# Seven products of a Strassen-like block product: matmuls alternate between two weight matrices and the halves of one PSUM bank

## The chip, the cores and the metric

The kernel runs on one core of a Trainium2 chip. The metric is the device time of one execution in microseconds (us). Two executions of the kernel before are shown: 1855.19 and 1855.77 us, median 1855.48 us. TensorE (PE) multiplies, ScalarE (ACT), VectorE (DVE) and GpSimd (POOL) do the elementwise work, and SyncE (SP) issues nearly all loads.

## The reference

A two-layer decoder trunk for 512 positions of width 1024 in float32. Each layer is a half-weighted SwiGLU block, a mixer (attention of three kinds), and another half-weighted SwiGLU block:

```
h = h + 0.5 * swiglu(rmsnorm(h, g[0]), w1, w3, w2)     # (silu(x @ w1) * (x @ w3)) @ w2
h = h + mixer(rmsnorm(h, g[1]))
h = h + 0.5 * swiglu(rmsnorm(h, g[2]), w1, w3, w2)
```

So there are four SwiGLU blocks. Their hidden width is 2816, which is 22 tiles of 128. The change lies in the products `x @ w1` and `x @ w3` of 18 of these 22 tiles.

## The kernel before

**Numbers.** Every float32 operand is split into a high part and a low part (fp32r), and each product is three matmuls: low weight by high input, high weight by low input, high weight by high input.

**Tiling of a SwiGLU block** (`ffn`, L628). The 22 hidden tiles come in three parts of 8, 8 and 6. After each part, eight second-layer units (`w2`) are multiplied (L366 to L368). The first four tiles of the first part go through `gate` (L439), with plain 512-column matmuls. The others are taken two at a time by `gates` (L562): a pair of tiles needs a two by two block product, which is done with seven smaller products in place of eight. So a block has 2 + 4 + 3 = 9 pairs, and the kernel has 36.

**One pair.** `sevens` (L519) loads four raw tiles, `one` and `two` for w1 and for w3 (L541, L542, both through L328), and makes the weights of the seven products from them. For w1 and then for w3: a11 with a12 (one 1024-wide split), a22 (a 512-wide split), then, after four additions at L533, s2 with s4, and s3 with s1 (1024-wide each). A split is a cast on ACT (L336) and a subtraction on DVE (L315), so a pair makes eight of each, in the order just told. The raw tiles and the split weights share 20 buffers, and a load on SP waits until its buffer is free.

**The seven products** (`product`, L571). In the order a11, a12, s2, s1, s3, s4, a22 each multiplies the weights of w1 into columns 0 to 255 of a PSUM bank and the weights of w3 into columns 256 to 511. Each half is one operation of the planner: 12 matmuls of 256 columns (four steps k of three). The bank is read (L594, L597) when both halves are done. `normed` (L458) makes the inputs of the products once for each block.

**What sets the order.** `Plan.emit` (L172) is a list scheduler that runs when the program is built. Each operation has an engine, a cost in ns, the tiles that it reads and writes, and a due value `v`; of the operations that could start soonest on an engine, the one with the smallest `v` goes next. An operation is offered only when all that it reads has been planned. The result is one fixed order for each engine; at run time every instruction waits for its own operands, and an engine runs its list strictly in order.

Of the kernel before, what the change touches and what calls it, by code (L numbers as in the profile page):

```python
# [103 lines left out]
def vec_ns(n):  # L104
    return n / 0.96 + 155


def sca_ns(n, extra=0):
    return n / 1.2 + 190 + 93 * extra
# [158 lines left out]
class Trunk:  # L268
# [293 lines left out]
    def gates(self, l, n, f, sx):  # L562


        nc, t = self.nc, self.t
        ws = self.sevens([(t[m][l, n, f], t[m][l, n, f + 1]) for m in ("w1", "w3")])
        pa, pb, pc = self.bank("sa"), self.bank("sb"), self.bank("sk")
        q1, q2 = Buf("d4", "cq2", (128, 1024)), Buf("d4", "cq2", (128, 1024))
        first, second = slice(0, 256), slice(256, 512)

        def product(ps, left, right, start):  # L571
            for m in range(2):
                w, c0 = ws[m][left]

                def g(m=m, w=w, c0=c0):
                    o = ps.t[:, m * 256:m * 256 + 256]
                    for k in range(4):
                        h, l, c, _ = sx[right][k]
                        at = slice(c0 + k * 128, c0 + k * 128 + 128)
                        wh, wl, xh, xl = w.at(0, at), w.at(1, at), h.t[:, c], l.t[:, c]  # L580
                        nc.tensor.matmul(o, wl, xh, start=start and m == 0 and k == 0, stop=False, skip_group_check=True)  # L581
                        nc.tensor.matmul(o, wh, xl, start=False, stop=False, skip_group_check=True)  # L582
                        nc.tensor.matmul(o, wh, xh, start=False, stop=k == 3, skip_group_check=True)  # L583
                keys = [key for x in sx[right] for key in x[3]]
                self.pe(12 * 117.5, g, self.parts(w) + keys, [ps])

        def view(q, c):
            return q.t.rearrange("p (m s) -> p m s", m=2)[:, :, c]

        def bank(ps):  # L590
            return ps.t.rearrange("p (m s) -> p m s", m=2)

        def copy(q, c, ps, key):
            self.act(sca_ns(S) - 40, lambda: nc.scalar.copy(view(q, c), bank(ps)), [ps], [(q, key)])  # L594

        def add(q, c, ps, key):
            self.dve(vec_ns(S), lambda: nc.vector.tensor_add(view(q, c), bank(ps), view(q, c)), [ps, (q, key)], [(q, key)])  # L597
        product(pa, "a11", "b11", True)
        copy(q1, first, pa, 0)
        product(pb, "a12", "b21", True)  # L600
        add(q1, first, pb, 0)
        product(pa, "s2", "t2", False)
        copy(q1, second, pa, 1)
        product(pc, "s1", "t1", True)
        copy(q2, second, pc, 1)
        product(pa, "s3", "t3", False)
        add(q2, second, pa, 1)
        product(pc, "s4", "b22", False)
        add(q1, second, pc, 1)
        product(pa, "a22", "t4", False)  # L610
        copy(q2, first, pa, 0)
        out = []
        for q, sign in ((q1, 1.0), (q2, -1.0)):
            g = self.s2("fa")
            gh, gl = self.s2("gt", F32R), self.s2("gt", F32R)
            self.act(sca_ns(S), lambda q=q, g=g, sign=sign: nc.scalar.activation(
                g.t, q.t[:, :512], AF.Silu, scale=sign), [(q, 0), (q, 1)], [g])
            if sign > 0:
                self.dve(vec_ns(S), lambda q=q, g=g: nc.vector.tensor_mul(g.t, g.t, q.t[:, 512:]), [g, (q, 0), (q, 1)], [g])
            else:  # L620
                self.dve(vec_ns(S), lambda q=q, g=g: nc.vector.scalar_tensor_tensor(
                    g.t, q.t[:, 512:], -1.0, g.t, op0=OP.mult, op1=OP.mult), [g, (q, 0), (q, 1)], [g])
            self.act(sca_ns(S), lambda g=g, gh=gh: nc.scalar.copy(gh.t, g.t), [g], [gh])
            self.sub(lambda gl=gl: gl.t, lambda g=g: g.t, lambda gh=gh: gh.t, [g, gh], [gl], S, ns=vec_ns)
            out.append((gh, gl))
        return out
# [695 lines left out]
```

## Time and profile before

| what | value |
|---|---|
| median of the two executions | 1855.48 us |
| the profiled execution, its own time | 1856.36 us |
| its span, first to last instruction | 1854.6 us |
| PE busy / DVE busy / ACT busy / POOL busy | 98% / 75% / 50% / 13% |
| mean granted TensorE clock | 0.99 of 2.4 GHz |
| matmuls at L581, L582, L583 | 2016 each, 128x256, 6048 in all |
| HBM traffic | 102 GB/s over the span |

A matmul's listed duration (about 283 ns) overlaps with the next ones; the distance between two starts is what one costs in a full stream. "Idle before" and "releaser" tell how long an engine stood still before an instruction and which event ended that. The profiled execution's own time is 1.8 us above its span and 0.9 us above the median.

### The profile page before, as it was taken

What the parts mean: (1) busy time and instruction counts of PE and PEld (TensorE: products, weight loads), DVE (VectorE), ACT (ScalarE), POOL (GpSimd) and SP (SyncE); (2) the same over time, 40 slices, a digit from 0 to 9 for tenths busy, and PEclk for the clock granted to TensorE, in tenths of its full rate; (3) what the DMA queues carried; (4) which work ended last, traced back from release to release, by engine and by line L of the source; (5) the groups of instructions that cost most, each with busy time, mean ns of one, the idle gap of its engine ahead of it and who ended that gap; (6) DMA issues with size and microseconds to landing.
All of it is one profiled execution on the core that took longest, in us unless ns stands there. A gap on an engine that the chain in (4) does not pass through costs nothing.

```text
span 1854.6 us, 28373 instructions
## 1 busy us (share of the span) xinstructions
PE 1811.5 (98%) x11174; PEld 1619.7 (87%) x11178; DVE 1398.2 (75%) x2222; ACT 936.2 (50%) x1558; POOL 245.1 (13%) x240
## 2 busy tenths in 40 slices
PE   8899999989999999999999999999999999999997
PEld 6789989867877789899998989989888889899896
DVE  7965866759998898487588965857789898567483
ACT  6443533636757746254264543525569655345153
POOL 1500001024622120010001000001023120010010
PEclk9899999999999999999999999999999999999999
DMA  6463233432222323234334223323412223243131
GB/s 210 121 207 101 84 101 106 126 103 77 87 59 78 93 71 121 62 108 132 91 103 125 69 91 103 125 70 103 137 60 69 86 80 95 78 124 126 60 112 46
DMA packets 65431, 185.45 MB, mean 100 GB/s; under 512 B 11985, under 2 KB 14769, under 8 KB 65297
## 3 DMA queue, kind: packets, MB, share of 16 engines
q1 hardware_dynamic: 58176, 176.88, 30.9%
q0 software_dynamic: 6688, 6.66, 1.3%
q8 instruction: 87, 1.43, 0.3%
q14 instruction: 48, 0.39, 0.1%
q10 hardware_dynamic: 432, 0.10, 0.0%
HBM read 179.81 MB, written 8.47 MB: 102 GB/s over the span
## 4 chain that ended last, share of the span: by engine, by line
PE 81%; DVE 12%; issue 2%; ACT 2%; DMA 2%; POOL 1%; SPq 1%; DVEq 0%; POOLq 0%; ACTq 0%
PE ps L581 12%; PE ps L582 12%; PE ps L583 12%; PE ps L366 11%; PE ps L367 11%; PE ps L368 11%; DVE d L315 3%; DVE s L315 2%; PE ps L837 1%; DMA d<-in_w 1%; PE ps L839 1%; PE ps L838 1%; PE ps L797 1%; DVE s L755 1%; DVE s L471 1%
## 5 line engine op out<-in xcount | busy, mean ns | idle before, releaser
L336 ACT CAST d<-d 128x1024 fp32r<-128x1024 f32 (+4 forms) x492 | 448.6, 927 | 405.0 <-DMA d<-in_w 223.3
L315 DVE TENSOR_TENSOR d<-d,d 128x1024 fp32r<-128x1024 f32 (+3 forms) x475 | 507.1, 1084 | 176.1 <-ACT d L336 155.0
L581 PE MATMUL ps<-s,d 128*128 128x256 f32 x2016 | 572.2, 284 | 10.9 <-DVE d L315 7.9
L582 PE MATMUL ps<-s,d 128*128 128x256 f32 x2016 | 571.5, 283 | 0.0
L583 PE MATMUL ps<-s,d 128*128 128x256 f32 x2016 | 571.4, 283 | 0.0
L366 PE MATMUL ps<-s,d 128*128 128x512 f32 x1188 | 471.8, 397 | 3.6 <-DVE d L315 3.6
L367 PE MATMUL ps<-s,d 128*128 128x512 f32 x1188 | 465.1, 392 | 0.2
L368 PE MATMUL ps<-s,d 128*128 128x512 f32 x1188 | 464.7, 391 | 0.0
L581 PEld LDWEIGHTS ps<-s,d 128*128 128x128 f32 x2016 | 388.0, 192 | 12.5 <-DVE d L315 8.2
L582 PEld LDWEIGHTS ps<-s,d 128*128 128x128 f32 x2016 | 388.0, 192 | 0.5
L583 PEld LDWEIGHTS ps<-s,d 128*128 128x128 f32 x2016 | 387.9, 192 | 0.0
L366 PEld LDWEIGHTS ps<-s,d 128*128 128x128 f32 x1188 | 224.4, 189 | 47.9 <-DVE d L315 3.8
L368 PEld LDWEIGHTS ps<-s,d 128*128 128x128 f32 x1188 | 224.0, 189 | 47.8
L367 PEld LDWEIGHTS ps<-s,d 128*128 128x128 f32 x1188 | 224.5, 189 | 42.9 <-DVE s L315 0.5
L594 ACT COPY d<-ps 128x512 f32<-128x512 f32 x144 | 84.4, 586 | 217.6 <-PE ps L583 217.5
L653 DVE SCALAR_TENSOR_TENSOR s<-ps,s 128x512 f32<-128x512 f32 x88 | 60.7, 690 | 137.0 <-PE ps L368 136.8
L315 DVE TENSOR_TENSOR s<-s,s 128x512 fp32r<-128x512 f32 (+2 forms) x188 | 148.7, 803 | 7.3 <-ACT s L372 2.1
L533 POOL TENSOR_TENSOR d<-d 128x512 f32<-128x512 f32 x18 | 23.6, 1313 | 937.1 <-DVE d L533 807.1
L597 DVE TENSOR_TENSOR d<-ps,d 128x512 f32<-128x512 f32 x108 | 73.5, 686 | 32.7 <-PE ps L583 32.1
L533 DVE TENSOR_TENSOR d<-d,d 128x512 f32<-128x512 f32 x133 | 87.5, 686 | 1.7
L533 DVE TENSOR_TENSOR d<-d 128x512 f32<-128x512 f32 x126 | 85.6, 695 | 2.2
L764 ACT ACTIVATE s<-s,stat 128x256 f32<-128x256 f32 (+3 forms) x128 | 65.9, 516 | 24.6 <-DVE stat L755 23.9
(147 smaller groups left out, 1872.0 us busy)
## 6 DMA issues: line engine op xcount, KB each, us to landing
d<-in_w SPq DMA_DIRECT2D x234, 512.0 KB, 3.7
d<-in_w SPq DMA_DIRECT2D x32, 384.0 KB, 3.2
d<-in_hyb_in SPq DMA_DIRECT2D x22, 512.0 KB, 3.9
d<-in_swa_in SPq DMA_DIRECT2D x10, 512.0 KB, 3.6
tab<-rv POOLq DMA_DIRECT2D x4, 1024.0 KB, 16.7
s<-tab SPq DMA_DIRECT2D x16, 256.0 KB, 4.0
d<-in_hyb_out SPq DMA_DIRECT2D x16, 256.0 KB, 2.9
d<-in_swa_out SPq DMA_DIRECT2D x16, 256.0 KB, 2.7
```

The source lines that it names most:

```text
L315: return lambda: eng.tensor_sub(out(), a(), b().bitcast(F32))
L336: alts = [("act", ns[0](n), lambda: nc.scalar.copy(hl.at(0, o), raw.t[:, c]))]
L366: nc.tensor.matmul(o, wl, xh.t, start=i == 0, stop=False)
L367: nc.tensor.matmul(o, wh, xl.t, start=False, stop=False)
L368: nc.tensor.matmul(o, wh, xh.t, start=False, stop=i == n - 1)
L533: return lambda: eng.tensor_add(o.t[:, oc], a.t[:, ac], o.t[:, oc])
L581: nc.tensor.matmul(o, wl, xh, start=start and m == 0 and k == 0, stop=False, skip_group_check=True)
L582: nc.tensor.matmul(o, wh, xl, start=False, stop=False, skip_group_check=True)
L583: nc.tensor.matmul(o, wh, xh, start=False, stop=k == 3, skip_group_check=True)
L594: self.act(sca_ns(S) - 40, lambda: nc.scalar.copy(view(q, c), bank(ps)), [ps], [(q, key)])
L597: self.dve(vec_ns(S), lambda: nc.vector.tensor_add(view(q, c), bank(ps), view(q, c)), [ps, (q, key)], [(q, key)])
L764: nc.scalar.activation(x, x, AF.Exp, bias=st.t[:, qb:qb + 1], scale=-1.0, accum_out=st.t[:, 4 + qb:5 + qb])
```

## The change

The two operations of a product become one of 24 matmuls. Within each step k, and for each of the three kinds, a matmul with w1 into the first half of the bank is followed by one with w3 into the second half. The number of matmuls, their shapes and operands stay. Each half still gets its 12 matmuls in the same order, and the flag that starts a bank stands on the first matmul alone, as before. The operation's cost is the sum of the two, and it reads the split weights of w1 and of w3.

```diff
         def product(ps, left, right, start):
-            for m in range(2):
-                w, c0 = ws[m][left]
-
-                def g(m=m, w=w, c0=c0):
-                    o = ps.t[:, m * 256:m * 256 + 256]
-                    for k in range(4):
-                        h, l, c, _ = sx[right][k]
-                        at = slice(c0 + k * 128, c0 + k * 128 + 128)
-                        wh, wl, xh, xl = w.at(0, at), w.at(1, at), h.t[:, c], l.t[:, c]
-                        nc.tensor.matmul(o, wl, xh, start=start and m == 0 and k == 0, stop=False, skip_group_check=True)
-                        nc.tensor.matmul(o, wh, xl, start=False, stop=False, skip_group_check=True)
-                        nc.tensor.matmul(o, wh, xh, start=False, stop=k == 3, skip_group_check=True)
-                keys = [key for x in sx[right] for key in x[3]]
-                self.pe(12 * 117.5, g, self.parts(w) + keys, [ps])
+            both = [ws[m][left] for m in range(2)]
+
+            def g():
+                for k in range(4):
+                    h, l, c, _ = sx[right][k]
+                    xh, xl = h.t[:, c], l.t[:, c]
+                    for a, x in ((1, xh), (0, xl), (0, xh)):
+                        for m, (w, c0) in enumerate(both):
+                            nc.tensor.matmul(ps.t[:, m * 256:m * 256 + 256], w.at(a, slice(c0 + k * 128, c0 + k * 128 + 128)), x,
+                                             start=start and m == 0 and k == 0 and a == 1, stop=k == 3 and a == 0 and x is xh,
+                                             skip_group_check=True)
+            keys = [key for x in sx[right] for key in x[3]]
+            self.pe(24 * 117.5, g, [key for w, _ in both for key in self.parts(w)] + keys, [ps])
```

## Rows read from the trace of the kernel before

**Rows 1.** Page, part 1: engine, busy us, share of the span, instructions.
```profile
PE 1811.5 (98%) x11174; PEld 1619.7 (87%) x11178; DVE 1398.2 (75%) x2222; ACT 936.2 (50%) x1558; POOL 245.1 (13%) x240
```

**Rows 2.** Page, part 4: the chain that ended last, share of span by engine.
```profile
PE 81%; DVE 12%; issue 2%; ACT 2%; DMA 2%; POOL 1%; SPq 1%; DVEq 0%; POOLq 0%; ACTq 0%
```

**Rows 3.** Page, part 5: line, operation, count, busy us, mean ns, idle before, releaser.
```profile
L581 PE MATMUL ps<-s,d 128*128 128x256 f32 x2016 | 572.2, 284 | 10.9 <-DVE d L315 7.9
...
L583 PE MATMUL ps<-s,d 128*128 128x256 f32 x2016 | 571.4, 283 | 0.0
```

**Rows 4.** Waits: who waited for whom, us in total, times, longest.
```profile
PE ps L581 <- DVE d L315: 7.9, 1, 7.9
```

**Rows 5.** Stretches: length, busy us (count) of PE, PEld, DVE, ACT, POOL, clock, DMA.
```profile
777.80:797.96 20.16, 20.16 (x170) 20.15 (x168) 8.62 (x13) 5.42 (x8) 1.30 (x1) 1.00 0.47 148
...
59.70:63.80 4.10, 4.10 (x22) 4.10 (x21) 3.50 (x6) 1.21 (x2) 1.50 (x3) 0.50 0.06 14
...
51.20:59.10 7.90, 0.05 (x1) 0.00 (x0) 6.63 (x9) 4.51 (x9) 7.75 (x7) 0.66 0.05 17
...
97.00:113.00 16.00, 14.29 (x113) 13.57 (x112) 9.48 (x12) 8.28 (x12) 0.74 (x1) 1.00 1.03 328
```

**Rows 6.** Timeline of PE (start us, us), a change of half and of bank.
```profile
779.12 0.28 PE L583 MATMUL ps<-s,d 128*128 128x256 f32 x1
779.24 0.28 PE L581 MATMUL ps<-s,d 128*128 128x256 f32 x1
...
780.56 0.28 PE L583 MATMUL ps<-s,d 128*128 128x256 f32 x1
780.68 0.28 PE L581 MATMUL ps<-s,d 128*128 128x256 f32 x1
```

**Rows 7.** Timeline of PE, the first pair of the kernel.
```profile
50.97 0.28 PE L583 MATMUL ps<-s,d 128*128 128x256 f32 x1
59.13 0.58 PE L581 MATMUL ps<-s,d 128*128 128x256 f32 x1 [7.88 <-DVE d L315]
...
59.94 0.41 PE L581 MATMUL ps<-s,d 128*128 128x256 f32 x1
...
63.13 0.41 PE L581 MATMUL ps<-s,d 128*128 128x256 f32 x1
```

**Rows 8.** Timeline of DVE, the same stretch.
```profile
57.87 1.21 DVE L315 TENSOR_TENSOR d<-d,d 128x1024 fp32r<-128x1024 f32 x1
```

**Rows 9.** Timeline of PE, second pair of a part: products s2 and s1 begin.
```profile
803.72 0.28 PE L581 MATMUL ps<-s,d 128*128 128x256 f32 x1
...
806.60 0.28 PE L581 MATMUL ps<-s,d 128*128 128x256 f32 x1
```

**Rows 10.** Timeline of DVE, the 1024-wide splits of the same pair's s-weights.
```profile
803.06 1.23 DVE L315 TENSOR_TENSOR d<-d,d 128x1024 fp32r<-128x1024 f32 x1 [0.52 <-ACT d L336]
...
804.80 2.35 DVE L315 TENSOR_TENSOR d<-d,d 128x1024 fp32r<-128x1024 f32 x2
```

**Rows 11.** Timeline of DVE and PE, first and last of the nine such pairs.
```profile
181.97 1.23 DVE L315 TENSOR_TENSOR d<-d,d 128x1024 fp32r<-128x1024 f32 x1 [0.52 <-ACT d L336]
182.63 0.28 PE L581 MATMUL ps<-s,d 128*128 128x256 f32 x1
...
1771.04 1.23 DVE L315 TENSOR_TENSOR d<-d,d 128x1024 fp32r<-128x1024 f32 x1 [0.51 <-ACT d L336]
1771.70 0.28 PE L581 MATMUL ps<-s,d 128*128 128x256 f32 x1
```

**Rows 12.** Timeline of PE, SP and POOL: a buffer's last reader, the load, its landing.
```profile
790.64 0.28 PE L583 MATMUL ps<-s,d 128*128 128x256 f32 x1
790.71 0.33 SPq L328 DMA_DIRECT2D d<-in_w  x1
794.64 1.30 POOL L533 TENSOR_TENSOR d<-d 128x512 f32<-128x512 f32 x1 [117.20 <-DVE d L533]
```

**Rows 13.** Waits of the SP queue: us in total, times, longest.
```profile
SPq L328 <- PE ps L583: 456.2, 100, 14.7
```

## The prediction

> **What bounds the kernel now.** I read the busy shares first: PE is busy for 1811.5 us of the 1854.6 us span, so 43 us are left in which it stands still [rows 1]. The chain of work that ended last agrees: 81% of it is PE and 12% is DVE [rows 2]. Then the costliest groups: the three lines that the change reorders issue 2016 matmuls each, 6048 in all, and L582 (its row is like that of L583) and L583 have no idle time before them; only L581, the first of each triple, shows 10.9 us [rows 3], most of it one wait of 7.9 us [rows 4]. So there are two ways to move the time: another distance between matmul starts in the stream, or other waits at the head of a product.
>
> The distance comes from the stretch table and not from the listed 284 ns, which overlap: one whole pair runs from 777.80 to 797.96, 20.16 us with 168 weight loads, 120.0 ns each, at a granted clock of 1.00 (2.4 GHz) [rows 5].
>
> **Part 1, the alternation itself.** Today's stream already holds the transitions that the change multiplies. At 779.12 to 779.24 the half of the bank and the weight matrix change together; the step is 0.12 us. At 780.56 to 780.68 the bank changes as well: 0.12 us again [rows 6]. All the others of that pair average the same 120.0 ns, though they write the columns that the matmul before them wrote. If writing the same half twice running cost anything, the change of half would be shorter; if changing the weight matrix cost anything, it would be longer. Neither is seen, and neither can hide in the next step, because the mean over 168 is exactly 120. So I cost this part at 6048 x 0 = 0 us.
>
> At the full clock the rows give 120.0 ns. The Trainium skill, page "TensorE: Matmul & The Clock Gate", section "Back-to-back issue gap", gives N/2.4 + 2.5 ns for an isolated warm matmul, an estimate of 109 ns for 256 columns; it also says that in a stream both the load and the matmul set the spacing. By the row this part is worth 0 us; by that formula, should alternating bring the stream there, 11 ns x 6048 = 67 us less, about 1789 us. The trace disagrees with the formula in this stream, by 11 ns a matmul, and shows no transition that gets nearer to it.
>
> **Part 2, both weights are needed at the start.** Today the w3 half of a product begins 12 x 0.12 = 1.44 us after the w1 half. Afterwards the second matmul needs w3, 0.12 us after the first: 1.32 us earlier. Behind it on PE, which runs in order, stands everything else. It costs only where w3's split is ready with less than 1.32 us in hand.
>
> The first pair of the kernel is the plain case. PE runs 24 matmuls up to 50.97 and then idles for 7.88 us, until 59.13, released by a DVE split [rows 7]. That split is 1024 wide and ends at 57.87 + 1.21 = 59.08 [rows 8]; it is w3's a11 with a12, since only w1's half of a11 and of a12 can have run before it. Afterwards nothing of these products can start before 59.08, and 24 x 0.12 = 2.88 us of PE work move behind the gap. The gap is 7.9 us today, with 0.05 us of PE work in it [rows 5], and would be about 11 us. The first 24 matmuls behind it run at half clock today (the granted clock is 0.50, 1.2 GHz, and the fifteen steps from 59.94 to 63.13 take 213 ns each [rows 5, 7]) and should do so again. Later PE idles again, for 16.00 - 14.29 = 1.71 us between 97 and 113 us, where the DMA engines are full (share 1.03) [rows 5]; a stretch that waits for loads can take back up to that. Ends: 0, if DMA sets the time there anyhow, and 2.88 + 24 x (0.213 - 0.120) = 5.1 us if nothing is taken back and the half clock lasts for 24 matmuls more. I take **1.5 us**, nearest to 2.88 - 1.71.
>
> The other places are the second pairs of a part: nine of them, one in each part that has three or four pairs (eight), and one in the first part of the last block, which has two. There product s2 begins at 803.72 and s1 at 806.60 [rows 9]. In the order of `sevens`, the split that ends at 803.06 + 1.23 = 804.29 is w3's s2 with s4, and the next two, up to 807.15, are s3 with s1 of w1 and of w3 [rows 10]. Today w3's half of s2 begins at 803.72 + 1.44 = 805.16, 0.87 us after its weights. Afterwards it wants them at 803.84, 0.45 us too early. The first and the last of the nine look alike: 183.20 against 182.63, 1772.27 against 1771.70 [rows 11].
>
> **Part 3, w1's buffers come free later.** Today the last read of w1's s3 is the twelfth matmul of its product, at 790.64; the load that waits for it goes out at 790.71 and POOL adds into what landed at 794.64 [rows 12]. Afterwards the last w1 read is the 23rd of 24. The product began 11 steps before 790.64, at 789.32, so that read is at 791.96, and the load goes out 1.32 us later. SP has 100 waits for L583 [rows 13], and loads queued behind this one move too. The landing feeds the four additions and the splits that end with w3's s2. How much of the 1.32 us arrives there, no row shows: nothing, if DVE and ACT work queued ahead of it sets the pace, or all of it. I take 0.95 us, nearer to all, because POOL starts as soon as the load lands. A second pair then waits 0.45 + 0.95 = 1.4 us at s2. At s1 it waits no more: w3's weights are there at 807.15 + 0.95 = 808.1, and the shifted product wants them at 806.72 + 1.4 = 808.1. Nine times 1.4 us is **12.6 us**; the ends are 9 x 0.45 = 4.1 us and 9 x (0.45 + 1.32) = 15.9 us, with 0 if the planner, which sees the same lateness in its own times, finds an order that hides it.
>
> What the edit removes besides, 252 planner operations with their waits, costs PE nothing today (steps of 0.12 us across them [rows 6]). In the pairs where weights lie ready for over 1.32 us, the cover is that lead; without it they would wait like the nine.
>
> **Sum.** 0 + 1.5 + 12.6 = 14.1 us on the profiled execution's 1856.4 us: 1870.5 us. It stands 0.9 us above the median of the runs shown, so on the median's scale 1869.6, rounded to 1870 us. By the ends: 1859.6 (0 + 4.1) to 1876.5 us (5.1 + 15.9).
>
> **Rivals.** *The waits are absorbed.* The planner moves the loads or casts of w3 ahead, or the chain to s2 in the nine pairs is paced by something that does not move. For it: DVE is idle for a quarter of the span. Against: the order of the splits is fixed by the order of their buffers. Time: 0 to 4 us over today, 1855 to 1859 us.
>
> *Alternation shortens the step.* If consecutive writes to one half held the stream up, the step could fall toward the pure streaming time: the 213 ns at half clock [rows 7] would be 106.5 ns at full clock. (120.0 - 106.5) x 6048 = 82 us, giving 1856.4 - 0.9 - 82 = 1774 us. Against it stand both transitions of rows 6. For it: only that a single change of half in twelve steps is a thin sample of a steady alternation.
>
> *The late release spreads to every pair, and the kernel is slower by more than 2%.* Place: the SP queue. If all 36 pairs have less than 1.32 us in hand once the loads of each go out 1.32 us later, each loses that much: 36 x 1.32 = 47.5 us, 1903 us. It decides from the point at which the lead of the third and later pairs falls under 1.32 us. For it: SP's 456 us of waiting for L583 [rows 13] say that loads follow PE closely. Against: a stall of PE delays the demand as well, so what DVE and the loads keep in hand grows by it.
>
> **How the numbers follow.** The forecast with its ends has 0.62; absorbed 0.20; the shorter step 0.06 (some of it too small to pass 2%); the spread release 0.08, half of it over 2%; 0.04 for an order of the planner that falls out otherwise, to either side. The range reaches down to the absorbed case with the scatter of an order that changes by a few us, and up just past the forecast's upper end: 1853 to 1878 us, which leaves out nearly 2 in 10. A difference of 2%, 37 us, is about what a measurement of this kernel can tell from no change; over 2% faster 0.05, within 0.90, over 2% slower 0.05.
>
> **What would show it.** Right: 120 ns between starts in the stream of a whole pair; PE idle from about 48 to 59 us; waits of about 1.4 us on a DVE split at the head of s2 in nine pairs, and loads that go out 1.3 us later in a product. Wrong: a step other than 120 ns decides at once for the second rival or its opposite; no new PE waits and a time near 1855 us for the first; waits in third and fourth pairs for the last.

## The result, and the profile after

The changed kernel takes 1886.84 us (median of 1886.62 and 1887.05) against 1855.48 us: ratio 1.0171, 95% interval 1.0146 to 1.0195. It is slower, as forecast, but by 31 us where 14 were forecast, and outside the range of 1853 to 1878 us. The profiled execution took 1886.62 us with a span of 1884.8 us, 30.2 us more than before.

Busy shares and the group of the products, from the page of the changed kernel (columns as in [rows 1, 3]; the three lines are now one, L580):

```profile
PE 1821.5 (97%) x11178; PEld 1626.0 (86%) x11178; DVE 1389.2 (74%) x2242; ACT 935.6 (50%) x1558; POOL 218.5 (12%) x220
...
L580 PE MATMUL ps<-s,d 128*128 128x256 f32 x6048 | 746.3, 286 | 30.9 <-DVE d L315 25.8
```

PE is busy 10 us longer and idle 20 us longer. Idle time in front of the products went from 10.9 us [rows 3] to 30.9 us. The waits of PE, where one wait of 7.9 us stood [rows 4]:

```profile
PE ps L580 <- DVE d L315: 25.8, 10, 10.7
...
PE ps L580 <- ACT d L593: 5.0, 16, 1.7
```

One whole pair without a wait, the next pair, and two stretches right behind the wait at s2, of that pair and of a similar one (columns as in [rows 5]):

```profile
786.62:806.78 20.16, 20.16 (x170) 20.15 (x169) 9.95 (x15) 5.93 (x9) 0.00 (x0) 1.00 0.34 116
806.78:830.92 24.14, 22.14 (x170) 21.73 (x169) 15.53 (x20) 9.26 (x13) 2.07 (x1) 0.93 0.32 98
814.60:817.30 2.70, 2.69 (x14) 2.69 (x15) 2.70 (x3) 0.80 (x1) 0.00 (x0) 0.61 0.75 228
...
943.25:945.95 2.70, 2.70 (x22) 2.70 (x23) 2.70 (x3) 0.79 (x1) 0.00 (x0) 1.00 0.60 183
```

The first row is the pair of [rows 5] again: 20.16 us for 168 matmuls that now alternate, 120.0 ns each (the counts in brackets take in those that overlap the ends of the stretch). The second is the pair of [rows 9, 10], 4.0 us longer. The third and fourth: behind the same wait the granted clock stays at 1.00 in one pair (22 matmuls listed) and averages 0.61 in the other (14).

In the pair at 806.78 s2 starts at 812.54. PE (start, us, idle before), then DVE, then ACT:

```profile
814.62 1.61 PE L580 MATMUL ps<-s,d 128*128 128x256 f32 x8 [1.80 <-DVE d L315]
...
809.76 0.69 DVE L533 TENSOR_TENSOR d<-d 128x512 f32<-128x512 f32 x1
811.14 0.69 DVE L620 SCALAR_TENSOR_TENSOR s<-d,s 128x512 f32<-128x512 f32 x1 [0.69 <-ACT s L615]
812.74 0.69 DVE L596 TENSOR_TENSOR d<-ps,d 128x512 f32<-128x512 f32 x1 [0.91 <-PE ps L580]
813.35 1.22 DVE L315 TENSOR_TENSOR d<-d,d 128x1024 fp32r<-128x1024 f32 x1
...
811.01 1.03 ACT L336 CAST d<-d 128x1024 fp32r<-128x1024 f32 x1
```

The cast of w3's s2 is done at 812.04, and DVE is idle. But its next instruction is L596, which reads the bank of a12 and waits until that product gives way to s2 at 812.54; the split stands behind it and ends at 814.57. PE's second matmul, due at 812.66, starts at 814.62: 1.96 us late. In the kernel before, the split ran ahead of that read (803.06 [rows 10]); the read came four microseconds later:

```profile
807.07 0.68 DVE L597 TENSOR_TENSOR d<-ps,d 128x512 f32<-128x512 f32 x1
```

The load of [rows 12] and a wait that the prediction did not have, that of product s4 in the pair after:

```profile
800.61 0.33 SPq L328 DMA_DIRECT2D d<-in_w  x1
...
845.04 0.59 ACT L593 COPY d<-ps 128x512 f32<-128x512 f32 x1 [3.75 <-PE ps L580]
...
845.68 0.50 PE L580 MATMUL ps<-s,d 128*128 128x256 f32 x2 [0.20 <-ACT d L593]
```

Product s3 began at 798.14, so the load goes out 2.47 us into it, where it was 790.71 - 789.32 = 1.39 us: 1.08 us later. In the next pair s1 gives way to s3 at 842.44, yet ACT copies its bank only at 845.04, and s4, which adds to that bank, starts 0.36 us late.

The first pair, with one matmul ahead of the gap where there were 24 [rows 7]:

```profile
48.42 0.28 PE L580 MATMUL ps<-s,d 128*128 128x256 f32 x1
59.37 2.93 PE L580 MATMUL ps<-s,d 128*128 128x256 f32 x12 [10.68 <-DVE d L315]
```

**Where the 30.2 us are**, from the starts of the products in both traces. The first two pairs cost 3.6 us. Eight second pairs cost 26.0 us: 2.5 us each in four of them (2.06 for the wait at s2 with its slow first step, 0.46 for s4) and 4.0 us in the four where the clock fell. Six other pairs lose 0.45 us at s4, 2.7 us. The ninth second pair waits 1.0 us at s2; with the pair ahead of it, which became shorter, it costs 0.7 us. Some 3 us come back, most of it in the first mixer, whose order shifted.

### The profile page after: what moved, and what is told of

The parts are those of the page before. It is cut to its first block, busy times and chain, and to the rows that moved or that the text cites. A ratio compares the mean times of both kernels' runs of the same rounds, so it can differ in the third digit from the quotient of the medians.

```text
span 1884.8 us, 28406 instructions
## 1 busy us (share of the span) xinstructions
PE 1821.5 (97%) x11178; PEld 1626.0 (86%) x11178; DVE 1389.2 (74%) x2242; ACT 935.6 (50%) x1558; POOL 218.5 (12%) x220
## 5 line engine op out<-in xcount | busy, mean ns | idle before, releaser
L580 PE MATMUL ps<-s,d 128*128 128x256 f32 x6048 | 746.3, 286 | 30.9 <-DVE d L315 25.8
L580 PEld LDWEIGHTS ps<-s,d 128*128 128x128 f32 x6048 | 740.1, 194 | 38.6 <-DVE d L315 28.3
L315 DVE TENSOR_TENSOR d<-d,d 128x1024 fp32r<-128x1024 f32 (+3 forms) x475 | 499.9, 1070 | 165.9 <-issue 110.6
L366 PEld LDWEIGHTS ps<-s,d 128*128 128x128 f32 x1188 | 224.1, 189 | 47.7 <-DVE d L315 4.0
L368 PEld LDWEIGHTS ps<-s,d 128*128 128x128 f32 x1188 | 223.6, 188 | 48.0
L367 PEld LDWEIGHTS ps<-s,d 128*128 128x128 f32 x1188 | 224.1, 189 | 41.9 <-DVE s L384 0.4
L315 DVE TENSOR_TENSOR s<-s,s 128x512 fp32r<-128x512 f32 (+2 forms) x188 | 138.2, 746 | 9.8 <-ACT s L622 4.4
L596 DVE TENSOR_TENSOR d<-ps,d 128x512 f32<-128x512 f32 x108 | 74.0, 686 | 81.3 <-PE ps L580 49.6
L533 POOL TENSOR_TENSOR d<-d,d 128x512 f32<-128x512 f32 x9 | 19.4, 2155 | 953.8 <-PE ps L580 825.2
L533 DVE TENSOR_TENSOR d<-d 128x512 f32<-128x512 f32 x144 | 96.2, 687 | 2.1
L780 POOL TENSOR_SCALAR s<-s,stat 128x256 f32<-128x256 f32 (+3 forms) x86 | 47.2, 564 | 130.6 <-DVE stat L773 111.4
L383 ACT ACTIVATE s<-s,gcol 128x512 fp32r<-128x512 f32 x48 | 34.3, 721 | 51.3 <-DVE s L652 30.7
L615 ACT ACTIVATE s<-d 128x512 f32<-128x512 f32 x72 | 43.9, 628 | 26.1 <-DVE d L596 25.8
L478 ACT CAST s<-s 128x512 fp32r<-128x512 f32 (+1 forms) x64 | 35.0, 564 | 35.6 <-DVE s L471 24.1
```

The costliest lines, as they stand in the source:

```text
L315: return lambda: eng.tensor_sub(out(), a(), b().bitcast(F32))
L366: nc.tensor.matmul(o, wl, xh.t, start=i == 0, stop=False)
L367: nc.tensor.matmul(o, wh, xl.t, start=False, stop=False)
L368: nc.tensor.matmul(o, wh, xh.t, start=False, stop=i == n - 1)
L533: return lambda: eng.tensor_add(o.t[:, oc], a.t[:, ac], o.t[:, oc])
L580: nc.tensor.matmul(ps.t[:, m * 256:m * 256 + 256], w.at(a, slice(c0 + k * 128, c0 + k * 128 + 128)), x, start=start and m == 0 and k == 0 ...
```

## The experiments

In all of these the arithmetic is complete; only the order of work differs. Each time stands beside the kernel before, run on the same chip; that one varies by 1.5 us from group to group, so differences between experiments are taken from what each adds to its own kernel before. In the diffs, `...` stands for lines that are not shown, and `kinds` for a list that the kernels write out in place.

**1. The merged operation alone.**

```diff
-                for k in range(4):
...
-                        for m, (w, c0) in enumerate(both):
+                for m, (w, c0) in enumerate(both):
+                    for k in range(4):
...
```

> One planner operation of 24 matmuls that reads both weights, as in the changed kernel, but its matmuls go through the first half of the bank and then the second, as before. Theory A (the fixed order on DVE that comes with the merged operation: the split of w3's s2 stands behind the DVE read of the bank of a12, which waits for the end of a12): the split is ready about 2.08 us after s2 starts, as in the changed kernel, but is wanted at 1.44 us, so eight pairs wait 0.64 us instead of 1.96: 10 us less for the waits, and up to 6 us less if the clock no longer falls: 1870 to 1876 us. Theory B (only the order of the matmuls costs: w3 wanted early, w1 released late): the time of the kernel before, 1855 to 1858 us. Theory C (the order of the planner costs everything, the order of the matmuls nothing): 1885 to 1888 us.

Measured: 1861.81 us against 1856.09, ratio 1.0033 (1.0020 to 1.0046). DVE and PE at s2, which starts at 803.95:

```profile
804.15 0.69 DVE L596 TENSOR_TENSOR d<-ps,d 128x512 f32<-128x512 f32 x1 [0.91 <-PE ps L580]
804.76 1.22 DVE L315 TENSOR_TENSOR d<-d,d 128x1024 fp32r<-128x1024 f32 x1
...
806.03 0.74 PE L580 MATMUL ps<-s,d 128*128 128x256 f32 x4 [0.48 <-DVE d L315]
```

The 13th matmul was due at 805.39 and starts 0.64 us late, in eight pairs, as theory A had it to the hundredth; s1 follows 0.2 us late (0.3 with its slow first steps). The clock no longer falls there, which theory A had. Yet the total is under its range, by two things that it did not have: the 14 waits at s4 (6.5 us with their slow first steps) went, and by the starts the first two pairs end 5.4 us earlier than in the changed kernel. Theory C fell: the planner's order costs 6 us when the halves follow each other. Theory B, the time of the kernel before, is missed by 4 us.

**2. The alternation alone, under the old plan.**

```diff
-            self.pe(24 * 117.5, g, [key for w, _ in both for key in self.parts(w)] + keys, [ps])
+            self.pe(12 * 117.5, lambda: None, self.parts(both[0][0]) + keys, [ps])
+            self.pe(12 * 117.5, g, self.parts(both[1][0]) + keys, [ps])
```

> The matmuls alternate as in the changed kernel, but the planner still sees two operations for each product (w1, then w3); the first issues nothing and the second all 24. The order of all engines is that of the kernel before. Theory A: the split of w3's s2 no longer stands behind the read of a12's bank; what is left is the lateness of 0.45 us that the trace of before shows, plus up to 1.32 us from the later release of w1's buffers, in nine pairs: 4 to 16 us, and up to 3 us in the first pair: 1859 to 1875 us. Theory B: all of the loss remains, 1884 to 1888 us. Theory C: 1855 to 1857 us. In all of them the step between matmuls in the stream stays 120 ns; if alternation changed it, this kernel would show it alone.

Measured: 1881.53 us against 1856.09, ratio 1.0136 (1.0119 to 1.0153). The range of theory A is missed by 6.5 us, that of theory B by 2.5; the greater part of the loss is there without the planner's new order. The waits of PE, and s2 of the second pair (start 815.66):

```profile
PE ps L580 <- DVE d L315: 21.7, 17, 10.7
...
PE ps L580 <- ACT d L594: 6.0, 8, 1.3
```
```profile
816.44 0.74 PE L580 MATMUL ps<-s,d 128*128 128x256 f32 x4 [0.51 <-DVE d L315]
```

By the starts: 11.2 us in 15 waits at the second matmul of s2 (0.66 us in the pair shown, which is typical; the longest is 1.55), 5.0 us in six waits at s3, where ACT had not yet read the bank, and 5 us in the first two pairs. So the order of the matmuls costs about 25 us under either plan (1881.5 - 1856.1, 1886.8 - 1861.8), and the plan about 6 under either order. The loss is not the queue on DVE alone: early need and late release cost it, and what they cost in a place depends on what the plan has put there.

**3. The read of a12's bank behind the split.**

```diff
-        add(q1, first, pb, 0)
+        add(q1, first, pb, 0, self.parts(ws[1]["s2"][0]))   # add() passes these on as further reads
```

> The changed kernel with one thing more: the DVE read of a12's bank is planned only after the split of w3's s2 (it names that split among what it reads). The matmuls and their waits are those of the changed kernel. Theory A: the split runs right after its cast, about 1.3 us earlier, and the wait at s2 falls from 1.96 to about 0.7 us in eight pairs: 10 us less, and up to 6 us more if the clock no longer falls: 1871 to 1877 us. Rival D (the late load of w3's second tile sets when the split is ready, and its place on DVE is of no account): unchanged, 1885 to 1888 us.

Measured: 1868.48 us, ratio 1.0069 (1.0054 to 1.0084). The same DVE list, s2 starting at 805.23, and PE:

```profile
804.77 1.23 DVE L315 TENSOR_TENSOR d<-d,d 128x1024 fp32r<-128x1024 f32 x1 [0.25 <-ACT d L336]
...
808.79 0.68 DVE L596 TENSOR_TENSOR d<-ps,d 128x512 f32<-128x512 f32 x1
...
806.05 1.21 PE L580 MATMUL ps<-s,d 128*128 128x256 f32 x8 [0.55 <-DVE d L315]
```

The split now starts as soon as its cast is done; PE's second matmul is 0.70 us late where it was 1.96, in seven of the eight pairs (1.56 in the other). It takes away 18 us, more than theory A's 10 to 16; by the starts 3.5 us of that lie in the first two pairs, which theory A left out. Rival D fell. The 14 waits at s4 stay (5.0 us).

**4 and 5. Late release and early need apart**, under the plan of the changed kernel. Only the last step k alternates (4), or only the first (5); the rest goes half by half.

```diff
-                for k in range(4):
...
+                kinds = ((1, 0), (0, 1), (0, 0))   # (low weight?, low input?)
+                for m, k, a, lo in ([(m, k, a, lo) for m in range(2) for k in range(3) for a, lo in kinds]
+                                    + [(m, 3, a, lo) for a, lo in kinds for m in range(2)]):        # experiment 4
...
+                for m, k, a, lo in ([(m, 0, a, lo) for a, lo in kinds for m in range(2)]
+                                    + [(m, k, a, lo) for m in range(2) for k in range(1, 4) for a, lo in kinds]):  # experiment 5
```

> The changed kernel's plan; of the four steps k the first three go through one half and then the other (nine matmuls with w1, nine with w3), only the last step alternates. So w1's buffers come free as late as in the changed kernel (its last low read is the 19th matmul, its last high read the 23rd), but w3 is wanted 1.08 us after the product starts. Theory N (the early need of w3 costs most): the wait at s2 falls from 1.96 to 1.0 us in eight pairs and the clock no longer falls behind it, 8 to 15 us less than the changed kernel: 1871 to 1879 us, with the waits of 0.36 us at s4 left as they are. Theory R (the late release of w1's buffers costs most, through loads and through reads of a bank that wait for a buffer): 1880 to 1887 us.

> The changed kernel's plan; only the first step k alternates, then come the other nine matmuls with w1 and then the other nine with w3. So w3 is wanted 0.12 us after the product starts, as in the changed kernel, but w1's last low read is the 13th matmul and its last high read the 15th. Theory N: the wait at s2 stays at 1.96 us in eight pairs (the split stands behind the read of a12's bank), the waits at s4 go: 1875 to 1881 us. Theory R: without the late release the time is that of the kernel with halves one after the other, 1861 to 1866 us.

Measured: (4) 1870.16 us against 1854.56, ratio 1.0083 (1.0069 to 1.0097); (5) 1876.64 us, ratio 1.0115 (1.0101 to 1.0129). PE at s2 and its waits for ACT, first of (4), which starts s2 at 805.87, then of (5), at 809.50:

```profile
807.94 1.33 PE L580 MATMUL ps<-s,d 128*128 128x256 f32 x9 [0.84 <-DVE d L315]
...
PE ps L580 <- ACT d L593: 5.4, 16, 1.7
```
```profile
811.58 0.67 PE L580 MATMUL ps<-s,d 128*128 128x256 f32 x2 [1.80 <-DVE d L315]
...
PE ps L580 <- ACT d L593: 2.2, 2, 1.7
```

In both, as in the changed kernel, w3's half begins 2.07 or 2.08 us after s2, whenever it was due: at 1.08 us, so 1.0 us late, and at 0.12 us, so 1.96 us late. The waits at s4 are there in (4), 14 times 0.36 us (14 of the 16 in its second row), and gone in (5). So they come from the late release, and the long waits at s2 from the early need. (5) lies in theory N's range, (4) a microsecond under it; theory R fell for both. Beyond what experiment 1 adds to its kernel before, early need adds 16 us in (5), where w1 is also freed three matmuls later, and late release with a quarter of the early need (0.36 of 1.32 us) 10 us in (4).

**6. The first pair's split ahead, on the kernel before.**

```diff
-            w = cut(a, 0, 1024, 0)
+            w = cut(a, 0, 1024, -25000 if v < 50000 else 0)
```

> The kernel before, with one due value changed: in the first pair of the kernel the splits of a11 with a12 are due 25 us earlier, so that w3's runs on DVE as soon as its cast is done and not behind the inputs of the products. If the idle 7.9 us in front of 59 us were only that one wait, 24 matmuls (2.9 us) move into it and the kernel takes 1851 to 1854 us. If DVE sets the time of the whole start, the split only pushes the inputs of the products back by its 1.2 us: 1855 to 1858 us.

Measured: 1861.47 us against 1854.56, ratio 1.0036 (1.0022 to 1.0050). Both expectations missed. The waits between 40 and 130 us:

```profile
ACT d L336 <- DMA d<-in_w: 19.5, 5, 9.8
...
PE ps L581 <- ACT d L594: 10.2, 3, 9.1
```

The small edit reordered the whole start: PE waits 9.1 us at once for a copy on ACT, whose list was held up by a cast that waits 9.8 us for a load: an instruction that PE waits for, queued behind another one, as in the changed kernel. Which step of the order put it there was not followed up.

**7 and 8. No early need.** Experiment 3's edit with the halves one after the other (7), and with twelve of the 24 matmuls in turns while w1 leads by two steps k (8).

```diff
+        add(q1, first, pb, 0, self.parts(ws[1]["s2"][0]))
...
+                for m, k, a, lo in ([(0, k, a, lo) for k in range(2) for a, lo in kinds]
+                                    + [(m, k + 2 - 2 * m, a, lo) for k in range(2) for a, lo in kinds for m in range(2)]
+                                    + [(1, k, a, lo) for k in range(2, 4) for a, lo in kinds]):     # experiment 8
```

> One planner operation, halves one after the other, and the DVE read of a12's bank planned after the split of w3's s2 (the third and the first experiment together). Theory: the split is ready about 0.8 us after s2 starts and wanted at 1.44 us, so none of the waits at s2 (5.1 us) and of those at s1 that follow from them (2.6 us) are left: 1853 to 1857 us. If the merged plan costs by something else, 1860 to 1863 us.

> The same plan, and matmuls that alternate between the halves for half of a product: w1 leads by two steps k (six matmuls), then twelve matmuls take turns, then w3 finishes alone. w3 is wanted at 0.72 us, when its s2 split is about ready, and w1's buffers come free at the 13th (low) and 17th matmul (high). Theory (alternation costs nothing, only what it asks for early and frees late): no wait over 0.1 us at s2 and none at s4, 1855 to 1861 us, and 120 ns a step in the stretch that alternates. If alternating as such cost something, half of it would be left here: 1865 us or more.

Measured: (7) 1852.45 us against 1855.16, ratio 0.9984 (0.9975 to 0.9993), a little below the kernel before; (8) 1855.67 us, ratio 1.0001 (0.9992 to 1.0010). The waits of PE, of (7) and then of (8): what is left at the products' line is the one wait of the first pair on DVE and, on ACT, one or two of 0.8 us and less, none of them in the nine second pairs. Then one whole pair of (8), 168 matmuls in 20.16 us at full clock, 120.0 ns each:

```profile
PE ps L580 <- DVE d L315: 9.4, 1, 9.4
PE ps L747 <- DVE s L315: 3.8, 3, 2.3
...
PE ps L580 <- ACT d L593: 0.8, 1, 0.8
```
```profile
PE ps L580 <- DVE d L315: 10.0, 1, 10.0
PE ps L747 <- DVE s L315: 4.6, 3, 3.1
...
PE ps L580 <- ACT d L593: 1.1, 2, 0.8
```
```profile
773.99:794.15 20.16, 20.16 (x170) 20.15 (x169) 9.95 (x15) 5.80 (x9) 0.00 (x0) 1.00 0.34 99
```

With half of the product in turns and little asked for early, the time is that of the kernel before. Against (7), which has the same plan and no turns, (8) takes 3.2 us more; about 2 us of that are steps of 0.21 to 0.22 us at s2 (eight pairs) and s4 (14 pairs), and where the rest lies is not shown. The step in the stream does not change. So alternation as such brings nothing, and what it costs is what it asks for early and frees late.

**The loss in two parts.** Each kernel against its own kernel before: with the read of a12's bank behind the split, full alternation adds 12 us (3) where halves one after the other save 3 (7), so the order of the matmuls costs 15 us by itself. With the read in front of the split, the same kernels add 31 us (the changed kernel) and 6 (1): the place of the read costs 19 us when the matmuls alternate and 8 when they do not.

## Why the prediction was wrong

**Part 1 was right.** In the whole stream of the changed kernel, the 5837 steps under 130 ns add up to 0.5 us less than 120 ns each would. The formula of the Trainium skill, page "TensorE: Matmul & The Clock Gate", section "Back-to-back issue gap" (109 ns by estimate for an isolated matmul of 256 columns) would have made the kernel faster; alternation brought no step of the stream there, at 120.0 ns before and after.

**Part 2, the first pair: right mechanism.** The gap of about 11 us came as written (10.68 us); the two first pairs cost 3.6 us where 1.5 were taken, inside the ends of 0 to 5.1.

**Part 2 and 3, the second pairs: the step that failed.** The prediction put the wait at s2 down to w3's weights being late by 0.45 us and by 0.95 of the 1.32 us of the load: 1.4 us. Places and sign were right. The size was not, for three reasons.

First, the order on DVE was carried over from the kernel before. The prediction said itself that the planner sees the lateness in its own times, but allowed for that as a gain and left 0.04 for an order that falls out otherwise. The planner put the read of a12's bank ahead of the split, and the split is then bound to the end of a12, just where s2 begins: 1.96 us, whatever the load does. Experiments 1, 4 and 5 show the same end of the split, about 2.08 us into s2, for three orders of matmuls, and experiment 3 shows 0.70 us without that read in front. That is the mechanism of the forecast alone, and there too its size was off: beside the 0.45 us it leaves 0.25 us for the later load, where the forecast took 0.95. Why the planner's own times put the read there was not followed up.

Second, late release was followed only through the load. It goes out 1.08 us later, not 1.32: the times 1.39 us (10th matmul of the product), 2.47 us (19th) and 1.75 us (13th, experiment 5) fit the last read of w1's low part (each is 0.31 us after that matmul starts), not the 12th matmul, a read of the high part, to which the prediction tied it. The other user of freed buffers is the result that ACT copies a bank into, and there the release cost 14 waits of 0.36 us at s4 that the sum did not have. Which buffer that copy takes, the trace does not name; that it is the release is shown by (5) against (4).

Third, the price of a wait was taken as its length. Behind it the first step took about 0.22 us in place of 0.12, and in four of eight pairs the granted clock fell; that made 8.2 us in 85 steps of 205 to 228 ns outside the first two pairs, against 0.1 us before.

**The rivals.** Absorbed waits did not come; experiments 7 and 8 show what it takes for them to. The shorter step fell. The spread release was wrong in its place (four third pairs and two first ones lose 0.45 us and not 1.32), but its kind, a release that reaches other users, was the part that the forecast lacked.

## What to carry to other kernels

Turning two groups of instructions into one that alternates leaves the work as it is but asks for the second group's operands at the start and frees the first group's buffers at the end; both have to be paid out of the lead that the trace shows for each, at every user of those buffers, loads and results alike. Where a scheduler makes the order, a change of one operation's size also changes what stands in front of whom on the other engines: look for an instruction that waits for the very work that waits for what is queued behind it. A wait on a full engine can cost more than its length: here 0.1 us for the first step behind it, and 1.5 us where the clock fell after it.

## What the runs showed of the hardware

The granted clock did not follow the length of the wait alone. In the changed kernel PE stood idle for about 1.8 us at the head of s2 in eight pairs, with the stream ahead of it at 2.4 GHz; in four of them it went on at 2.4 GHz, in the other four the clock fell to 1.2 GHz for some of the steps behind it (0.61 granted over 2.70 us in one of them), at 1.5 us a pair. In experiment 5, with the same eight stretches of 1.8 us, it fell in two. With shorter ones (experiments 1, 3 and 4: idle for 0.48, 0.55 and 0.84 us in the pairs shown, and once for 1.4 us in experiment 3) all eight kept the clock. What decides among equal waits, no run shows.
